# A fp32 decoder trunk: contiguous compression operand, all weight pieces split by engines, eight pair tiles and four raw tiles

## The chip, the core and the metric

One core of a Trainium2 chip runs the whole kernel in one launch. The metric is the device time in microseconds (us) of one execution. The engines are named as in the profile: PE (TensorE, the matmuls), PEld (its weight loads), DVE (VectorE), ACT (ScalarE), POOL (GpSimd) and SP (SyncE, which here only issues transfers). Each engine works through its own queue of instructions in the order in which they were written; one that waits holds up all behind it on that engine.

## The reference, cut to what matters

The input is one sequence of 256 tokens with 1024 features, all in fp32. Two layers follow one another, each a token mixer and an MLP.

```python
for i in range(DEPTH):                       # DEPTH = 2
    h = _rmsnorm(x, norm_mix[i])
    x = x + (_rglru_mixer(h, ...) if i % 2 == 0 else _nsa_mixer(h, ...))
    h = _rmsnorm(x, norm_ffn[i])
    x = x + _sq_relu_mlp(h, mlp_w_up[i], mlp_w_down[i])
return _rmsnorm(x, norm_final)
```

The first mixer is recurrent (projections, a short convolution, gates, a scan). The second is sparse attention with 16 heads in 4 groups. It has three branches: a compressed one, a selected one and a sliding window. The compressed keys and values come from blocks of 32 tokens, taken every 16 tokens, which gives 15 blocks:

```python
def _compress(z, pe, w1, w2):
    blocks = blocks + pe[None, None, :, None, :]          # a learned offset per position in the block
    flat = ...reshape(B, nc, G, CMP_LEN * DH)             # 32 x 64 numbers per block and group
    return jax.nn.gelu(flat @ w1, approximate=True) @ w2
```

## The kernel before, in words

Activations lie with features on the 128 partitions and the 256 tokens along the free axis. Every large product is made of three matmuls (`mm3`, L327 to L330): weight and activation are each split into a high part in fp32r and a low part, the rounding rest, and high by high, high by low and low by high are summed in a PSUM bank. So every weight must be split before use.

**Pieces.** The weights come as pieces of 128 x 1024 numbers (512 KB), in the order of `weight_pieces`. A piece is loaded from HBM into one of NRAW = 5 raw tiles (`load`, L274, on SP's queue), copied into the high half of one of NSPL = 7 pair tiles (`whl`) by ACT or DVE, and then the low half is written by DVE as raw minus high, a "diff" here (L297 in the MLPs, L333 elsewhere). PE consumes a piece with 24 matmuls. A raw tile is free after the diff, a pair after PE's last matmul of that piece. Eight pieces (`BY_DMA`: q3, kw1, q5, q7, o01, o03, o11, o13) go another way (`split_dma`): POOL's queue loads the piece into the high half (L388), ACT or DVE writes its negative into the low half (L390), and a second load on POOL's queue adds the raw weight to that (L392). They are read from HBM twice and need no raw tile.

**Order.** The two mixers, with the norms around them, are written as tasks (`Plan.add`): engine or engines that may do it, a duration, what it reads and writes. `Plan.plan` makes a list schedule from priorities, improves it with passes forwards and backwards, and `emit` writes the instructions in the order of the planned starts. `SEEDS` holds, for each mixer, the seeds that disturb the priorities. So the order on every engine follows from a table of numbers and the durations in the code. The MLPs are written by hand: at each of their 64 pieces a `tick` makes the diff of one piece and the high copy of the next, up to 6 pieces ahead of PE.

**The attention section** runs from the statistics of the norm (L434 to L445) to those of the next norm. Its pieces are, in order, ks0 kw0 q0 q1 (keys and queries), ck0 ck1 cv0 cv1 (inputs of the compression), q2, five pieces of values, q3 ks1 kw1 q4 q5 q6 q7, and o00 to o13 (output). A projection (`proj`, 24 matmuls) is multiplied by the norm's factor into a scratch tile `tt`. Keys and queries of ks0, kw0, q0, q1 and q2 are split straight into their places by ACT and DVE; those of the others are split into `th`/`tl` and carried to other partitions by transfers of 64 KB on SP's queue (`move`, L364). Then come, head by head, `scores` (L1149, L1150), the exponentials on ACT (L1159), `rescale` (L1178), `transposes` (L1189) with their split into `pth` (ACT, L1192) and `ptl` (DVE, L1193), and for every two heads `pv` (L1214, L1216, L1221), whose result goes through `osum` (ACT L1225, DVE L1228) to the output projection. There are eight of these pv steps. Every stage has work on PE, ACT and DVE.

**The compression.** `cproj` (L943) copies the scaled projection into a tile `zf`: for each of 15 blocks and 4 groups, 16 positions, with the two halves of the block on the two halves of the partitions. This is done by 16 transfers on SP's queue (tile `zwoh` in the profile). Two more transfers fetch the learned offset as column 60 of each half (L931). `hidden` then multiplies with `w1` (tile `zwol`): 16 matmuls over 122 columns (L957), one per position `l`. `zf` is stored with the position innermost, so that the 122 columns of `zf[:, :, l]` lie 16 numbers (64 bytes) apart. `hidden` goes on with a short chain on ACT and DVE (L963 to L971), whose result `hid` the matmuls L978 and L997 need. `zf` and `w1` lie in the space that the attention's outputs `oh` and `ol` take later.

## Time and profile before

Three runs took 584.11, 585.10 and 585.17 us. One execution was profiled.

| what | us |
|---|---|
| median of the three runs | 585.1 |
| profiled execution | 583.35 |
| its span, first to last instruction | 581.6 |
| recurrent mixer, to the second statistics | about 95 |
| first MLP | about 173 |
| attention section, from 267.6 to 404.8 | 137.2 |
| second MLP and the final norm | about 177 |

The profile lists, for each engine, when it was busy, by line and tile, and what ended its idle time. Times in views are us from the start of the span. In the views by stretch of time, each engine's busy time is followed by its number of instructions. A DVE or ACT instruction is shown from its start to its end, and the next may start some 0.1 us before that end, so the step from start to start in a full queue is a little shorter than the duration shown.

### The profile page before, as it was taken

Reading aid. Unit: us, or ns where it says so; the run is one execution under the profiler, and the core shown is the slowest. Engines: PE = TensorE matmul, PEld = TensorE weight load, DVE = VectorE, ACT = ScalarE, POOL = GpSimd, SP = SyncE. Lnnn points to the kernel's source line nnn. Section 1 sums busy time; section 2 is a strip of 40 time slices with the busy share of each in tenths; the row PEclk is TensorE's granted clock in tenths of the full one; section 3 lists DMA queues with packets and bytes.
Section 4 is the critical chain, followed back from the end, with each engine's and each line's share of the span. In section 5 each row is a group of like instructions: output and inputs, shape, how many; then the busy total and the mean of one; then the engine's idle time right before and its main releaser. Section 6 shows DMA issues by size and latency. Waiting matters only on the chain.

```text
span 581.6 us, 12202 instructions
## 1 busy us (share of the span) xinstructions
PE 568.7 (98%) x4766; PEld 559.3 (96%) x4766; DVE 416.3 (72%) x859; ACT 356.9 (61%) x715; POOL 54.4 (9%) x69
## 2 busy tenths in 40 slices
PE   9999999999999999999999999999999999999994
PEld 9999999999999999999999988989999999999994
DVE  6999998776775646648749989999867766464522
ACT  7699776666564434437528999987866654443410
POOL 1110000000001113111011100000000000232320
PEclk9999999999999999999999999999999999999998
DMA  8936466565665664665597776333766667466302
GB/s 295 382 126 206 142 224 223 185 206 186 191 207 186 204 220 158 205 219 202 130 308 176 162 187 173 133 74 98 254 193 190 199 193 240 160 194 229 122 1 72
DMA packets 34761, 108.39 MB, mean 186 GB/s; under 512 B 4592, under 2 KB 8576, under 8 KB 34704
## 3 DMA queue, kind: packets, MB, share of 16 engines
q1 hardware_dynamic: 31776, 98.61, 52.1%
q0 software_dynamic: 2352, 8.49, 6.8%
q8 instruction: 37, 0.61, 0.4%
q10 hardware_dynamic: 576, 0.53, 0.3%
q14 instruction: 20, 0.16, 0.1%
HBM read 103.48 MB, written 1.05 MB: 180 GB/s over the span
## 4 chain that ended last, share of the span: by engine, by line
PE 88%; ACT 5%; DVE 4%; DMA 2%; issue 1%; POOL 0%; DVEq 0%; ACTq 0%; POOLq 0%
PE bank L329 27%; PE bank L328 27%; PE bank L330 27%; PE bank L689 2%; ACT pt L1159 2%; DMA whl<-in_dram 2%; ACT pt L1178 1%; PE bank L574 1%; PE bank L1189 1%; ACT pth L1192 1%; DVE whl L333 1%; DVE ptl L1193 1%; DVE pt L1156 1%; PE bank L1149 0%; PE bank L1150 0%
## 5 line engine op out<-in xcount | busy, mean ns | idle before, releaser
L328 PE MATMUL bank<-hhl,whl 128*128 128x256 f32 x768 | 215.0, 280 | 0.2 <-DVE tt L893 0.2
L329 PE MATMUL bank<-hhl,whl 128*128 128x256 f32 x768 | 212.6, 277 | 0.0
L330 PE MATMUL bank<-hhl,whl 128*128 128x256 f32 x768 | 212.4, 277 | 0.0
L297 DVE TENSOR_TENSOR whl<-raw,whl 128x1024 fp32r<-128x1024 f32 x118 | 147.5, 1271 | 2.8 <-ACT whl L288 2.8
L328 PEld LDWEIGHTS bank<-hhl,whl 128*128 128x128 f32 x768 | 144.2, 188 | 0.7 <-DVE tt L893 0.4
L329 PEld LDWEIGHTS bank<-hhl,whl 128*128 128x128 f32 x768 | 144.3, 188 | 0.5 <-DVE hhl L582 0.2
L330 PEld LDWEIGHTS bank<-hhl,whl 128*128 128x128 f32 x768 | 144.2, 188 | 0.0
L328 PE MATMUL bank<-uhl,whl 128*128 128x256 f32 x512 | 141.4, 276 | 0.0
L330 PE MATMUL bank<-uhl,whl 128*128 128x256 f32 x512 | 141.3, 276 | 0.0
L329 PE MATMUL bank<-uhl,whl 128*128 128x256 f32 x512 | 141.3, 276 | 0.0
L288 ACT CAST whl<-raw 128x1024 fp32r<-128x1024 f32 x119 | 121.2, 1041 | 23.4 <-issue 18.8
L329 PEld LDWEIGHTS bank<-uhl,whl 128*128 128x128 f32 x512 | 96.1, 188 | 0.0
L330 PEld LDWEIGHTS bank<-uhl,whl 128*128 128x128 f32 x512 | 96.1, 188 | 0.0
L328 PEld LDWEIGHTS bank<-uhl,whl 128*128 128x128 f32 x512 | 96.1, 188 | 0.0
L532 DVE TENSOR_TENSOR xt<-xt,bank 128x256 f32<-128x256 f32 x40 | 16.1, 416 | 84.5 <-PE bank L330 84.4
L333 DVE TENSOR_TENSOR whl<-raw,whl 128x1024 fp32r<-128x1024 f32 (+3 forms) x64 | 66.3, 1058 | 3.9 <-ACT whl L336 3.9
L784 ACT ACTIVATE u<-t 128x256 f32<-128x256 f32 x64 | 26.7, 418 | 57.3 <-DVE t L779 54.1
L336 ACT CAST whl<-raw 128x1024 fp32r<-128x1024 f32 (+3 forms) x57 | 52.6, 947 | 11.1 <-DMA raw<-in_dram 6.7
L779 DVE SCALAR_TENSOR_TENSOR t<-bank,rstd 128x256 f32<-128x256 f32 x64 | 26.9, 423 | 45.3 <-PE bank L330 44.8
L1317 ACT ACTIVATE xg<-xt,vec 128x256 f32<-128x256 f32 x8 | 4.1, 509 | 47.9 <-DVE xt L532 47.9
L1159 ACT ACTIVATE pt<-pt,mx 128x256 f32<-128x256 f32 (+1 forms) x64 | 28.6, 450 | 3.4 <-DVE mx L1156 3.3
L508 ACT ACTIVATE hhl<-xt,vec 128x256 fp32r<-128x256 f32 x8 | 4.1, 510 | 39.3 <-DVE xt L532 39.3
(207 smaller groups left out, 821.0 us busy)
## 6 DMA issues: line engine op xcount, KB each, us to landing
raw<-in_dram SPq DMA_DIRECT2D x167, 512.0 KB, 4.3
whl<-in_dram POOLq DMA_DIRECT2D x16, 512.0 KB, 5.7
gw<-in_dram SPq DMA_DIRECT2D x4, 512.0 KB, 9.0
raw<-in_dram SPq DMA_DIRECT2D x5, 256.0 KB, 4.7
xt<-in_dram SPq DMA_DIRECT2D x4, 256.0 KB, 4.5
zwol<-in_dram SPq DMA_DIRECT2D x2, 512.0 KB, 6.3
zwoh<-tt SPq DMA_DIRECT2D x16, 60.0 KB, 2.3
raw<-in_dram SPq DMA_DIRECT2D x2, 456.0 KB, 4.9
```

Of the source, the lines that this page charges most:

```text
L288: (act.copy if eng is None else eng.tensor_copy)(hi_t[i % NSPL][:, :n], raw_t[i % NRAW][:, :n])
L297: (eng or dve).tensor_tensor(lo[:, :n], raw_t[i % NRAW][:, :n], hi[:, :n].bitcast(F32), op=OP.subtract)
L328: pe.matmul(ps, wh, xh, start=start, stop=False)
L329: pe.matmul(ps, wh, xl, start=False, stop=False)
L330: pe.matmul(ps, wl, xh, start=False, stop=stop)
L333: return lambda e: e.tensor_tensor(o, a, h.bitcast(F32), op=OP.subtract)
L336: return lambda e: (e.copy if e is act else e.tensor_copy)(o, a)
L532: dve.tensor_tensor(xt[:, m], xt[:, m], z, op=OP.add)
L689: e.matmul(z(), gw[b][:, o:o + P], xb[2 * b + k], start=k == 0, stop=k == 1)
L779: dve.scalar_tensor_tensor(t, z, 0.0, rs, op0=OP.max, op1=OP.mult)
L784: act.activation(u, t, AF.Square)
L1159: add("act", (0.39, 0.49)[qc], lambda e, row=row, j=j: e.activation(row, row, AF.Exp, bias=mx[:, j:j + 1], scale=-1.0, accum_out=sm[:, j:j ...
```

## The change

- `zf` is stored with the block innermost: the 122 columns that a matmul of `hidden` reads lie side by side. The 16 transfers of `cproj` become copies on ACT or DVE, whose writes are now 122 numbers apart, and the two transfers of the learned offset become copies on POOL.
- `BY_DMA` and `split_dma` are gone: all pieces are loaded on SP's queue and split by ACT and DVE.
- Four raw tiles instead of five, eight pair tiles instead of seven. Two pieces, q3 and ks1 (`LENT`), get no pair: their halves lie in the `oh` and `ol` tiles, which the compression has left by then and pv needs later. The scratch tiles `tt`, `gx` and `gy` are replaced by tiles that exist already.
- The planner knows transfers as a task on SP that issues (0.6 us) and a task on one "dma" resource that carries them in the order of issue; of its three best plans it takes the one whose replay, with queues in fixed order, ends PE first. Two costs in `stats` are raised, and both tables of seeds are new.

```diff
-NRAW, NSPL = 5, 7
+NRAW, NSPL = 4, 8
...
-BY_DMA, DLEAD, NPEN = "q3 kw1 q5 q7 o01 o03 o11 o13", 8.0, 0.3
-MLAG = (3.4, 4.0)
+LENT = "q3 ks1".split()
+TRANSFER = {"raw": (2.0, 1.4, 0.6), "move": (1.4, 0.21, 0.3)}
...
-FIRST = "x0+ 00 01 x2+ 10+ 20+ x4+ 02+ x6+ 12+ 22+ piece vec cst piece"
+FIRST = "x0+ 00 01 x2+ 10+ 20+ x4+ 02+ x6+ 12+ 22+ piece vec cst"
...
     def plan(self, prio):
         plans = [self.list_schedule(prio, 0.1)]
         for _ in range(ROUNDS):
             plans.append(self.forwards(self.backwards(*plans[-1])))
-        return min(plans, key=lambda p: max(p[0].values()))
+        plans.sort(key=lambda p: max(p[0].values()))
+        return min(plans[:3], key=lambda p: self.replay(*p))
...
-        while state["dma"] <= min(i + 4, len(order) - 1):
+        while state["dma"] <= min(i + NRAW - 1, len(order) - 1):
...
+        def transfer(self, kind, q, d, fn, t, r=(), w=()):
+
+            pre, took, post = TRANSFER[kind]
+            self.add(q, d, fn, r=r, w=list(w) + ["loads"] * (kind == "raw"), t=t, lag=pre)
+            self.plan.carried[len(self.plan.tasks)] = len(self.plan.tasks) - 1
+            self.add("dma", took, lambda e: None, r=r, w=w, t=t, lag=post)
...
-                if j in by_dma:
-                    continue
-                self.add("sp", 1.5, lambda e, j=j: load(j), w=[("raw", j % NRAW), "loads"], t=t - 20 + j * 1e-3, lag=2.0)
+                self.transfer("raw", "sp", 0.6, lambda e, j=j: load(j), t - 20 + j * 1e-3, w=[("raw", j % NRAW)])
...
-        def split_dma(self, i, n, hi, lo, t):
-
-            src = wts[offs[i]:offs[i + 1]].rearrange("(p n) -> p n", p=P)
-            hk, lk = [("hi", i % NSPL)], [("lo", i % NSPL)]
-            self.add("pool", 0.6, lambda e: e.dma_start(hi, src), w=hk, t=t - DLEAD, lag=4.8)
...
+        def slot(self, i):
+
+            if home[i] >= 0:
+                return hi_t[home[i]], lo_t[home[i]], [("hi", home[i])], [("lo", home[i])]
+            b = home[i] + 2
+            return Lent("oh", b), Lent("ol", b), [("oh", 4 * b + j) for j in range(4)], [("ol", 4 * b + j) for j in range(4)]
...
-        tt = many([P, S], F32, "tt", 3)
+        tt, ttk = [acc, *sqs], ["acc", ("sq", 0), ("sq", 1)]
...
-        zf = zw[0][:, :2 * ZW * 16].rearrange("p (z l) -> p z l", l=16)
+        zf = zw[0][:, :2 * ZW * 16].rearrange("p (l z) -> p z l", l=16)
...
-            add("sp", 0.5, lambda e, i=i, c=pecol: e.dma_start(zf[:, ZW * i + 60], vec_in[:, c:c + 16]), r=zok,
-                w=[("z", i, "p")], t=W1T, lag=2.0)
+            add("pool", 0.15, lambda e, i=i, c=pecol: e.tensor_copy(zf[:, ZW * i + 60], vec[:, c:c + 16]), r=zok + ["vec"],
+                w=[("z", i, "p")], t=-5)
...
-                    dst = zf[own_(j), ZW * i + g * NB:ZW * i + (g + 1) * NB].rearrange("p n l -> p (n l)")
-                    sec.move(dst, x[own_(hf), j * 16:j * 16 + 240], [xk] + zok, [("z", i, g, j)], t + 0.5, "sp")
+                    dst = zf[own_(j), ZW * i + g * NB:ZW * i + (g + 1) * NB]
+                    y = x[own_(hf), j * 16:j * 16 + 240].rearrange("p (n l) -> p n l", l=16)
+                    add(HI, copy(dst, y), r=[xk] + zok, w=[("z", i, g, j)], t=t + 0.5)
```

Three places show how the order moves. The first is SP's queue in the first third of the attention section. `raw` tiles receive weights, `zwoh` is the tile of `zf`, `sa`, `sb`, `kh` and `kl` are queries and keys that are carried from `th` and `tl`. Before:

```order
L274 DMA raw_79<-in_dram 128x1024
L364 DMA zwoh<-tt_3227 64x240 x4
L364 DMA zwoh<-tt_3225 64x240 x4
L364 DMA zwoh<-tt_3226 64x240 x4
L364 DMA zwoh<-tt_3227 64x240 x4
L274 DMA raw_81<-in_dram 128x1024
L274 DMA raw_78<-in_dram 128x1024
```

After the change, at the same place:

```order
L312 DMA raw_80<-in_dram 128x1024
L312 DMA raw_81<-in_dram 128x1024
L312 DMA raw_78<-in_dram 128x1024
L415 DMA sb_3217<-th_3223 64x256
L415 DMA sa_3213<-th_3223 64x256
L415 DMA sb_3217<-tl_3225 64x256
L415 DMA sa_3213<-tl_3225 64x256
L415 DMA kh<-th_3224 64x256 x4
L312 DMA raw_79<-in_dram 128x1024
```

The 16 transfers into `zwoh` are gone; loads of raw weights follow one another up to the first transfers of queries.

The second place is PE's queue around the 16 matmuls of `hidden` (L957, now L1004). `bank_3608` and `bank_3623` hold values before, `bank_3565` holds the projection q2 after. Before:

```order
L1019 MATMUL bank_3608<-whl,hhl 128x304
L1020 MATMUL bank_3608<-whl,hhl 128x304
L1021 MATMUL bank_3608<-whl,hhl 128x304
L957 MATMUL bank_3652<-zwoh,zwol 128x122 x16
L1019 MATMUL bank_3623<-whl,hhl 128x304
L1020 MATMUL bank_3623<-whl,hhl 128x304
```

After:

```order
L366 MATMUL bank_3565<-hhl,whl 128x256
L367 MATMUL bank_3565<-hhl,whl 128x256
L368 MATMUL bank_3565<-hhl,whl 128x256
L1004 MATMUL bank_3593<-zwoh,zwol 128x122 x16
L366 MATMUL bank_3565<-hhl,whl 128x256
L367 MATMUL bank_3565<-hhl,whl 128x256
```

Ahead of `hidden`, PE had all of q2 (24 matmuls), 30 matmuls of values and five pairs of score matmuls before; now it has 18 matmuls of q2, none of values and four pairs of scores. The seven projections ahead of q2 stand there as before.

The third place is ACT's queue where `hidden` has ended (`cb`, L963, now L1010). Before:

```order
L336 CAST sa_3214<-tt_3225 64x256
L336 CAST whl<-raw_81 128x1024
L963 COPY cb<-bank_3652 64x1 x2
L336 CAST whl<-raw_78 128x1024
L969 ACTIVATE gy<-gy 128x60
```

After:

```order
L374 CAST whl<-raw_79 128x1024
L1206 ACTIVATE pt,sm_3246<-pt,mx_3242 128x128
L374 CAST oh<-raw_80 128x1024
L1010 COPY cb<-bank_3593 64x1 x2
L374 CAST sb_3216<-acc 64x256
L374 CAST sa_3212<-acc 64x256
L1016 ACTIVATE cs_3250<-cs_3250 128x60
```

The high half of a lent piece is written to `oh`, the tile of `zf`, right ahead of `cb`, and no cast of a piece stands between `cb` and the tanh (L969, now L1016).

More of the change, by code (lines that the diff above doesn't have):

```diff
@@ L118, in lag @@
         lag = self.tasks[i][4]
-        if lag is not None and not by == e == "sp":
+        if lag is not None and by != e:
             return lag
@@ L218, in priorities, with replay @@
         return prio
+    def replay(self, end, by, dur, work=lambda i, e, d: d, wait=lambda i, l: l):
+        queues = {e: [] for e in self.engines}
+        for i in sorted(end, key=lambda i: (round(end[i] - dur[i], 6), i)):
+            queues[by[i]].append(i)
+        carrier = {u: i for i, u in self.carried.items()}
+        free, done, head = dict(self.busy), {}, {e: 0 for e in queues if e != "dma"}
+        ready = dict.fromkeys(head)
+        while True:
+            for e, r in ready.items():
+                if r is None and head[e] < len(queues[e]):
+                    i = queues[e][head[e]]
+                    if all(k in done for k in self.tasks[i][2]):
+                        ready[e] = max([free[e]] + [done[k] + wait(k, self.lag(k, by[k], e)) for k in self.tasks[i][2]]), e, i
+            left = [r for r in ready.values() if r]
+            if not left:
+                break
+            t, e, i = min(left)
+            ready[e] = None
+            head[e] += 1
+            free[e] = done[i] = t + work(i, e, dur[i])
+            if i in carrier:
+                u = carrier[i]
+                t = max([free["dma"]] + [done[k] + wait(k, self.lag(k, by[k], "dma")) for k in self.tasks[u][2]])
+                free["dma"] = done[u] = t + work(u, "dma", dur[u])
+        assert len(done) == len(end)
+        return max(t for i, t in done.items() if by[i] == "pe")
     def plan(self, prio):
@@ L262, in trunk_kernel @@
     state = {"dma": 0, "split": 0, "lo": 0, "get": 0}
+    home, lent, n = {}, {}, 0
+    for i, x in enumerate(order):
+        if x[0] + str(x[1]) in LENT:
+            home[i] = LENT.index(x[0] + str(x[1])) % 2 - 2
+        else:
+            home[i], n = n % NSPL, n + 1
     WMAX = 1024
@@ L341, in trunk_kernel, with __init__, __getitem__ @@
     piece_no = {n: i for i, n in enumerate(order)}
-    by_dma = {piece_no[x[:-1], int(x[-1])] for x in BY_DMA.split()}
+    class Lent:
+        def __init__(self, name, b):
+            self.name, self.b = name, b
+        def __getitem__(self, at):
+            return lent[self.name](self.b)[at]
     class Section:
@@ L407, in ahead @@
             for i in range(g, min(g + n, len(order))):
-                self.add("pe", 2.58, lambda e: None, r=[("hi", i % NSPL), ("lo", i % NSPL)] + ["rs"] * (i - g >= 2),
+                self.add("pe", 2.58, lambda e: None, r=[("hi", home[i]), ("lo", home[i])] + ["rs"] * (i - g >= 2),
                          w=["next"], t=t + step * (i - g))
-            self.load(g + n + 3, t)
+            self.load(g + n + NRAW - 2, t)
         def bank(self, key, b, view):
@@ L674, in gate_load @@
             o = offs[-1] + b * P * 1024
-            add("sp", 1.5, lambda e: e.dma_start(gw[b], wts[o:o + P * 1024].rearrange("(p n) -> p n", p=P)), w=[("gw", b), "loads"],
-                t=t, lag=2.0)
+            sec.transfer("raw", "sp", 0.6, lambda e: e.dma_start(gw[b], wts[o:o + P * 1024].rearrange("(p n) -> p n", p=P)), t,
+                         w=[("gw", b)])
         def gate(b, t):
@@ L854, in trunk_kernel, with lend @@
         oh, ol = (lambda i, n=n: opart(n, i) for n in ("oh", "ol"))
+        def lend(n):
+            return lambda b: (opart(n, 0), ohl[n][:, b * WMAX:(b + 1) * WMAX])[1]
+        lent.update({n: lend(n) for n in ("oh", "ol")})
         ptht, ptlt = (at.tile([P, NTH * 3 * P], F32R, name=n) for n in ("pth", "ptl"))
@@ L924, in trunk_kernel @@
         hid = pre.tile([P, 4, NCP], F32, name="hid")
-        gx, gy = (pre.tile([P, 60], F32, name=n) for n in ("gx", "gy"))
         GELU1, GELU3 = float(np.sqrt(2.0 / np.pi)), 0.044715
@@ L959, in hidden @@
             t += 3
-            x, y, k2 = gx, gy, ["gx"]
+            (x, y), k2 = (c.rearrange("p j q n -> p (j q n)")[:, :60] for c in css), [("cs", 0), ("cs", 1)]
             for i in range(2):
```

52 lines of the change are left out of this document (23 added, 29 removed).

## The prediction

> **What bounds the kernel now.** I read the page first, then the stretches of the attention section, then what VectorE and SP wait for in it.
>
> ```profile
> span 581.6 us, 12202 instructions
> PE 568.7 (98%) x4766; PEld 559.3 (96%) x4766; DVE 416.3 (72%) x859; ACT 356.9 (61%) x715; POOL 54.4 (9%) x69
> ```
>
> PE is busy in 98% of the span, so only the stages in which it waits, or does slow work, can give anything. Busy time by stretch, PE first, then PEld, DVE, ACT and POOL:
>
> ```profile
> 30.00:60.00 30.00, 30.00 (x216) 28.55 (x215) 29.51 (x49) 29.56 (x54) 2.11 (x5) 1.00 0.52 173
> 105.00:245.00 140.00, 140.00 (x1238) 140.00 (x1237) 89.67 (x120) 72.50 (x112) 13.15 (x11) 1.00 0.60 196
> 267.60:305.00 37.40, 36.94 (x279) 36.30 (x276) 24.82 (x60) 19.83 (x47) 3.46 (x5) 1.00 0.79 240
> 305.00:390.10 85.10, 81.72 (x615) 75.42 (x616) 80.50 (x315) 79.67 (x245) 8.54 (x15) 1.00 0.60 149
> 390.10:404.80 14.70, 14.70 (x131) 14.67 (x131) 14.45 (x33) 9.74 (x21) 0.00 (x0) 1.00 0.33 96
> 410.00:568.00 158.00, 158.00 (x1396) 158.00 (x1396) 92.56 (x122) 77.78 (x121) 18.76 (x13) 1.00 0.57 177
> ```
>
> In the MLPs (second and last row) a matmul takes 140/1238 = 0.113 us, PE never rests, and DVE has a third of its time free. They give nothing. The three rows between them are the attention section: 137.2 us, cut where `hid` is made (305.0) and where the last pv has left `osum` (390.1). From 305 on, DVE rests 85.1 - 80.5 = 4.6 us, ACT 5.4 us and PE 3.4 us: all three are nearly full and wait on each other in turn. Ahead of 305, DVE rests 12.6 us. Where this rest lies, by DVE's own stretches, and what ends it:
>
> ```profile
> 281.00:289.80 8.80, 6.59 (x19) 1.00 0.44 92
> 289.80:305.00 15.20, 6.57 (x14) 1.00 1.02 317
> ```
>
> ```profile
> 276.51 0.33 SPq L274 DMA_DIRECT2D raw<-in_dram  x1
> 278.26 11.44 SPq L364 DMA_DIRECT2D zwoh<-tt  x16
> 289.80 2.67 SPq L274 DMA_DIRECT2D raw<-in_dram  x5
> ```
>
> ```profile
> DVE whl L390 <- DMA whl<-in_dram: 5.8, 2, 5.5
> ```
>
> From 276.5 to 289.8 SP issues only the 16 transfers of the compression; no weight is loaded, and then five loads and those of POOL come at once. In the last 15.2 us DVE works 6.57 us; 5.8 us of its rest are one wait for a piece that POOL's queue loads.
>
> **The change, part by part.** All terms are taken against the profiled execution, 583.35 us with a span of 581.6; it lies 1.75 us under the median of 585.1, and I add the same difference to the median.
>
> *The operand of `hidden`.*
>
> ```profile
> L957 PEld LDWEIGHTS bank<-zwoh,zwol x32: 192/206/207, 293.8 to 300.1; 128*128 128x128 f32 x32
> L957 PE MATMUL bank<-zwoh,zwol x32: 372/384/386, 293.9 to 300.3; 128*128 128x122 f32 x32
> L689 PE MATMUL bank<-xb,gw x64: 378/379/379, 27.2 to 47.0; 128*128 128x256 f32 x64
> L997 PE MATMUL bank<-w2raw,pt x8: 218/275/275, 306.9 to 307.6; 128*128 128x64 f32 x8
> ```
>
> The 16 matmuls are 32 records, (300.3 - 293.9)/31 = 0.206 us each. For a contiguous fp32 operand there are two rows: 256 columns end 0.379 us after their start, as late as these 122; and 64 columns follow one another in 0.7/7 = 0.10 us. So 122 contiguous columns should take between 0.10 and some 0.12 us; I take 0.11, and 32 x (0.206 - 0.11) = 3.1 us leave PE. The bounds are 2.7 and 3.4.
>
> [...]
>
> *The copies into `zf`.* There are 16, ten on ACT and six on DVE by the order.
>
> ```profile
> L336 ACT COPY pt<-hid 128x128 f32<-128x128 f32 x2 | 0.6, 293 | 0.0
> L336 DVE COPY pt<-hid 128x128 f32<-128x128 f32 x2 | 0.4, 220 | 0.0
> ```
>
> The nearest copies have 128 numbers per partition, these 240. I take 0.32 us on ACT and 0.27 on DVE: 3.2 and 1.6 us. They can't cost less than the quoted rows, and with writes at twice the price they cost 6.4 and 3.2. The last of them stand between cv1's projection and `hidden`: one on ACT, three on DVE. Meanwhile PE has a pair of scores and 18 matmuls of q2, 2.2 us. At my price DVE needs 0.4 + 3 x 0.27 = 1.2 us, and PE doesn't wait; at twice the price it takes 2.0 and is just in time.
>
> *Eight pieces by engines.* Eight more diffs on DVE. The eight negations (L390, five on ACT, three on DVE) become eight high copies of about the same length.
>
> ```profile
> 363.30 1.14 DVE whl L333
> ...
> 368.87 1.14 DVE whl L333
> ```
>
> ```profile
> L390 ACT ACTIVATE whl<-whl x5: 1047/1052/1064, 310.9 to 353.8; 128x1024 fp32r<-128x1024 f32 x5
> L390 DVE TENSOR_SCALAR whl<-whl x3: 679/695/699, 291.8 to 382.5; 128x1024 fp32r<-128x1024 f32 x3
> ```
>
> DVE: 8 x 1.14 = 9.1 more, 1.6 of copies, 3 negations of 0.6 less, and 1.2 less since the order gives small copies to ACT: +7.7 us. By the order there are 10 diffs before `hid` in both kernels, then 7 before and 15 now up to the last pv, then 4 in both. So about 0.2 of this falls ahead of `hid` and 7.5 between `hid` and the last pv. ACT gets about +6.8, of which 4 after `hid`: 79.7 + 4 = 83.7, less than DVE's 88.0. DVE is the one to watch.
>
> *How early `hid` is made.* PE's order puts L957 ahead of 30 matmuls of values (0.14 us each, 4.2), 6 of q2 (0.7) and a pair of scores (0.2). It starts at 293.9 - 5.1 = 288.8 and ends 16 x 2 x 0.11 = 3.5 later, at 292.3. What follows `hidden` before:
>
> ```profile
> 301.68 1.05 ACT L336 CAST whl<-raw 128x1024 fp32r<-128x1024 f32 x1 [0.59 <-ACT cb L963]
> ```
>
> ```profile
> 301.86 0.70 DVE L390 TENSOR_SCALAR whl<-whl 128x1024 fp32r<-128x1024 f32 x1 [5.51 <-DMA whl<-in_dram]
> 302.47 0.57 DVE L965 TENSOR_SCALAR gx<-bank,cb 64x60 f32<-64x60 f32 x2
> ...
> 303.47 1.22 DVE L333 TENSOR_TENSOR whl<-raw,whl 128x1024 fp32r<-128x1024 f32 x1
> ...
> 305.00 0.21 DVE L971 SCALAR_TENSOR_TENSOR hid<-gy,gx 128x60 f32<-128x60 f32 x1
> ```
>
> From L965 to the end of L971 it was 2.7 us with a diff of 1.2 in between; now two diffs of 0.34 stand there, so 2.2. Ahead of it ACT now writes the lent piece into `oh`, which must wait for `hidden` to leave that space: 1.0 us, and 0.3 for `cb`. So `hid` comes at 292.3 + 0.1 + 1.0 + 0.3 + 2.2 = 295.9. Counted from 267.6 that is 28.3; I take 28.5 instead of 37.4. DVE has 24.8 + 0.2 = 25.0 us of work there, so it fits, with 3.5 us of rest instead of 12.6.
>
> *Transfers.* The wait for L390 goes, 4 MB are read less, and the 16 transfers no longer stand ahead of loads on SP. In the middle, one stall is a queue of transfers:
>
> ```profile
> 339.00:348.00 9.00, 7.73 (x61) 7.23 (x60) 7.34 (x24) 8.03 (x23) 1.42 (x2) 1.00 0.59 133
> ```
>
> ```profile
> 338.85 0.24 PE bank L1189 x3
> 339.08 1.79 DMA sb<-th
> 340.87 0.28 DVE th L336
> ...
> 341.83 0.53 PE bank L1189 x3
> ```
>
> Here DVE rests 9.0 - 7.34 = 1.7 us of its 4.6. With POOL's loads gone and transfers planned in the order of issue I let this one go: 2.9 us of rest remain.
>
> *Four raw tiles, eight pairs, borrowed tiles.* At nothing, since loads stay far ahead:
>
> ```profile
> L297 DVE TENSOR_TENSOR whl<-raw,whl 128x1024 fp32r<-128x1024 f32 x118 | 147.5, 1271 | 2.8 <-ACT whl L288 2.8
> ...
> raw<-in_dram SPq DMA_DIRECT2D x167, 512.0 KB, 4.3
> ```
>
> ```profile
> DMA to landing us min/median/max: 3.1/4.3/11.0
> ```
>
> In an MLP load i+3 starts when diff i-1 is done (1.27 after tick i) and must land by tick i+3, 3 x 24 x 0.113 = 8.1 us after tick i. That leaves 6.9 us for a landing of 4.3, and PE is up to six pieces behind the splits. If the cover went, each piece would cost the excess. The recurrent mixer is planned anew on engines that are 98% busy (first row of stretches); PE never waits there before, so it can only lose: 0 to 1 us, I take 0.
>
> **The sum.** DVE's work and rest fill the section: 28.5 to `hid`, then 80.5 + 7.5 + 2.9 = 90.9, then 14.5 as before: 133.9 instead of 137.2, 3.3 us less. PE alone would allow 133.4 - 3.1 = 130.3. Profiled 580.05, median **581.8 us**. One measurement of this kernel can tell about 0.2%, 1.2 us, from no change.
>
> **The rivals.** *PE stays the bound.* The new order packs DVE without rest and `hid` comes in time: only PE's 130.3 counts, 6.9 us less, 578.2. For it: all the diffs that were added have pieces loaded early. Against it: PE, ACT and DVE then need 95% and more of the same time.
>
> *A wait takes the place of the old ones.* The stall of 339 is replaced by another, since eight more loads share SP's queue with the 64 KB transfers (rest 4.6), and the copies into `zf` at twice the price bring `hid` to 30: 30 + 88.0 + 4.6 + 14.5 = 137.1, no change, 585.0. [...]
>
> *Four raw tiles are too few* (slower). A tile's round is landing, high copy (1.05), diff (1.2). With four tiles it must stay under 4 x 2.71 = 10.8, so it decides at a landing of 8.5 us. The longest landing is 11.0; at 9.6 each piece costs 0.25 us, and 25 diffs up to the last pv cost 6.3: 3 us slower than before with the gain of 3.3 taken off, 588.1. For it: DMA share 1.02 in 289.8 to 305. Against it: this crowd came from loads held back by the 16 transfers, and the median is 4.3.
>
> **How the numbers follow.** Forecast 0.45; PE the bound 0.23; another wait 0.17; four tiles 0.15. The forecast's own range is 580.4 to 583.5 (a rest of 1.5 to 4.6 us behind the same `hid`), all of it faster by over 0.2%. So faster 0.68, same 0.17, slower 0.15. The range of 577.5 to 586.3 leaves out most of the slower case and the best end of PE's.
>
> **What would show it.** L1004's records at about 0.11 us; `hid` at about 296; no load held back between 276 and 290; DVE resting 2 to 4 us from `hid` to the last pv, the section 134 long, the MLPs unchanged. I am wrong if PE's rate in the MLPs changes, if `hid` comes after 300, or if DVE rests more than 6 us behind it.

## The result, and the profile after

The changed kernel takes 592.84 us (median, 592.52 to 594.71), the kernel before 584.61 (583.60 to 585.17) on the same chip: a ratio of 1.0149, with a 95% interval of 1.0137 to 1.0161. It is 8.2 us slower, where 2.8 to 3.3 us faster was forecast. The profiled execution after took 593.09 us, with a span of 591.3; the one before has 581.6. So 9.7 us are to be found between the two traces, 1.5 us more than between the medians, since the profiled execution before (583.35 us) is a short one.

The page of the changed kernel, its first lines:

```profile
span 591.3 us, 12174 instructions
PE 569.8 (96%) x4766; PEld 559.6 (95%) x4766; DVE 428.3 (72%) x869; ACT 366.8 (62%) x729; POOL 43.2 (7%) x55
```

PE was busy in 98% of the span before, now in 96%: it waits for 21.5 us instead of 12.9. Where the time went can be cut at ACT's copy of rstd, which opens each section (start of the last three of its four copies, us from the span's start):

| | 2nd (MLP 0) | 3rd (attention) | 4th (MLP 1) | span |
|---|---|---|---|---|
| before | 95.1 | 267.9 | 404.9 | 581.6 |
| after | 99.8 | 274.1 | 414.5 | 591.3 |
| lost up to here | 4.7 | 6.3 | 9.6 | 9.7 |

The recurrent mixer lost 4.7 us, the step from there into the attention 1.6, the attention 3.3 and the rest nothing. The same stretches of the changed kernel that the prediction quoted of the kernel before, and two more at the starts of sections (busy time of PE, PEld, DVE, ACT and POOL, then granted clock, DMA share and GB/s):

```profile
24.40:30.00 5.60, 4.54 (x36) 4.24 (x36) 5.54 (x19) 3.75 (x8) 0.98 (x3) 1.00 1.02 415
105.00:245.00 140.00, 140.00 (x1238) 140.00 (x1237) 90.70 (x127) 75.79 (x123) 11.30 (x10) 1.00 0.61 199
268.00:274.50 6.50, 4.18 (x35) 3.80 (x33) 2.31 (x4) 3.17 (x5) 0.79 (x3) 1.00 0.66 213
274.50:305.00 30.50, 29.33 (x231) 28.83 (x231) 26.83 (x60) 23.90 (x52) 0.00 (x0) 0.94 0.49 152
305.00:397.00 92.00, 88.26 (x665) 82.25 (x664) 88.08 (x322) 86.41 (x257) 1.63 (x4) 1.00 0.38 110
397.00:414.50 17.50, 16.02 (x120) 15.47 (x121) 14.40 (x32) 9.81 (x22) 0.00 (x0) 0.90 0.45 154
```

The MLP's rate is unchanged (1238 matmuls in 140 us). `hid` is made 30.5 us behind rstd instead of 37, as hoped, but the stretch behind it grew from 85.1 to 92.0 and the tail from 14.7 to 17.5. PE is the engine to follow: in the attention it was busy for 36.94 + 81.72 + 14.70 = 133.4 us before, and for 29.33 + 88.26 + 16.02 = 133.6 now, although the operand of `hidden` saves it 3 us. The granted clock, third from the right in a row, tells why: 0.94 over 30.5 us and 0.90 over 17.5 us leave 1.8 + 1.8 = 3.6 us of full clock missing, an estimate from these rows. Without that PE's work would be 130.0 us, close to the 130.3 that the prediction has for PE alone. The rest of the loss is waits: PE rests for 140.0 - 133.6 = 6.4 us of the section, 3.8 before. The operand does what it should:

```profile
L1004 PE MATMUL bank<-zwoh,zwol x32: 275/275/343, 297.4 to 300.9; 128*128 128x122 f32 x32
```

(300.9 - 297.4)/31 = 0.113 us for one record instead of 0.206. The largest new wait is at the attention's start. ACT's instructions there, first before, then after:

```profile
267.86 0.37 ACT L445 COPY rstd<-bank 128x256 f32<-128x256 f32 x1 [0.76 <-PE bank L529]
268.72 2.33 ACT L336 CAST kh<-tt 64x256 fp32r<-64x256 f32 x6 [0.49 <-DVE tt L893]
271.08 1.05 ACT L336 CAST whl<-raw 128x1024 fp32r<-128x1024 f32 x1
```

```profile
269.85 0.26 ACT L484 ACTIVATE rcol<-bank,epst 128x2 f32<-128x2 f32 x1 [0.25 <-PE bank L567]
273.19 1.05 ACT L374 CAST whl<-raw 128x1024 fp32r<-128x1024 f32 x1 [3.08 <-DMA raw<-in_dram]
274.14 0.36 ACT L488 COPY rstd<-bank 128x256 f32<-128x256 f32 x1
```

Now a high copy of a weight piece stands between the root and the copy of rstd. It is q2's piece, which is multiplied only behind the eight projections of the compression, but ACT works its queue in order: it waits 3.08 us for that piece, and rstd waits with it. Why the piece is late stands in the waits of SP's queue between 262 and 275 (total, times, longest), and in the landing times of line 312 between 264 and 276:

```profile
SPq L312 <- DVE whl L335: 7.2, 1, 7.2
...
DMA to landing us min/median/max: 4.0/5.4/6.9
```

The transfer itself took 4.0 us. It was issued only at 269.1, since SP waited 7.2 us for a diff to free the tile. Before, a load waited as long between 255 and 275, but no high copy that needs it stood ahead of rstd:

```profile
SPq L274 <- DVE whl L297: 10.7, 4, 7.2
```

Behind rstd hang VectorE (its timeline, first fence) and then PE, which gets a lower clock when it comes back (stretches, second fence):

```profile
274.54 0.42 DVE L940 TENSOR_TENSOR sq<-bank,rstd 128x256 f32<-128x256 f32 x1 [4.23 <-ACT rstd L488]
```

```profile
275.00:277.00 2.00, 1.99 (x9) 1.99 (x10) 2.00 (x2) 1.61 (x4) 0.00 (x0) 0.50 0.59 227
397.40:400.00 2.60, 2.52 (x11) 2.33 (x12) 2.21 (x4) 1.40 (x3) 0.00 (x0) 0.58 0.45 178
```

Nine matmuls in 2.0 us, 0.22 us each, at a granted clock of 0.50. The second row lies behind the other large wait, the one behind the last pv. PE's timeline there, first before, where nothing waits, then after:

```profile
388.49 0.40 PE L1221 MATMUL bank<-pc,bhl 128*128 128x256 f32 x2
388.72 0.28 PE L328 MATMUL bank<-oh,whl 128*128 128x256 f32 x1
```

```profile
394.95 0.40 PE L1268 MATMUL bank<-pc,bhl 128*128 128x256 f32 x2
397.40 0.38 PE L366 MATMUL bank<-oh,whl 128*128 128x256 f32 x1 [2.04 <-DVE oh L374]
```

### The profile page after: what moved, and what is told of

Same layout as the page of the kernel before. It is cut to its first block, busy times and chain, and to the rows that moved or that the text cites. A ratio compares the mean times of both kernels' runs of the same rounds, so it can differ in the third digit from the quotient of the medians.

```text
span 591.3 us, 12174 instructions
## 1 busy us (share of the span) xinstructions
PE 569.8 (96%) x4766; PEld 559.6 (95%) x4766; DVE 428.3 (72%) x869; ACT 366.8 (62%) x729; POOL 43.2 (7%) x55
## 4 chain that ended last, share of the span: by engine, by line
PE 81%; ACT 7%; DVE 6%; DMA 4%; issue 1%; SPq 0%; DVEq 0%; ACTq 0%
PE bank L366 24%; PE bank L367 24%; PE bank L368 24%; DMA raw<-in_dram 3%; PE bank L732 2%; ACT pt L1206 2%; ACT whl L374 1%; ACT zwoh L374 1%; ACT pt L1225 1%; PE bank L1236 1%; PE bank L1263 1%; DVE whl L371 1%; PE bank L1004 1%; ACT pth L1239 1%; DMA vec<-in_dram 1%
## 5 line engine op out<-in xcount | busy, mean ns | idle before, releaser
L366 PE MATMUL bank<-hhl,whl 128*128 128x256 f32 x752 | 211.3, 281 | 2.8 <-DVE sq L940 2.8
L367 PE MATMUL bank<-hhl,whl 128*128 128x256 f32 x752 | 209.0, 278 | 3.2 <-DVE hhl L625 2.6
L368 PE MATMUL bank<-hhl,whl 128*128 128x256 f32 x752 | 208.7, 278 | 0.0
L367 PEld LDWEIGHTS bank<-hhl,whl 128*128 128x128 f32 x752 | 142.0, 189 | 4.0 <-DVE hhl L625 2.8
L366 PEld LDWEIGHTS bank<-hhl,whl 128*128 128x128 f32 x752 | 142.0, 189 | 3.3 <-DVE sq L940 3.0
L368 PEld LDWEIGHTS bank<-hhl,whl 128*128 128x128 f32 x752 | 141.9, 189 | 0.0
L371 DVE TENSOR_TENSOR whl<-raw,whl 128x1024 fp32r<-128x1024 f32 (+3 forms) x70 | 74.1, 1074 | 4.1 <-ACT whl L374 3.8
L374 ACT CAST whl<-raw 128x1024 fp32r<-128x1024 f32 (+3 forms) x60 | 57.8, 971 | 14.9 <-DMA raw<-in_dram 12.2
L1206 ACT ACTIVATE pt<-pt,mx 128x128 f32<-128x128 f32 (+1 forms) x64 | 28.7, 451 | 2.8 <-DVE mx L1203 2.5
```

What stands on the lines that cost most here:

```text
L366: pe.matmul(ps, wh, xh, start=start, stop=False)
L367: pe.matmul(ps, wh, xl, start=False, stop=False)
L368: pe.matmul(ps, wl, xh, start=False, stop=stop)
L371: return lambda e: e.tensor_tensor(o, a, h.bitcast(F32), op=OP.subtract)
L374: return lambda e: (e.copy if e is act else e.tensor_copy)(o, a)
L1206: add("act", (0.39, 0.49)[qc], lambda e, row=row, j=j: e.activation(row, row, AF.Exp, bias=mx[:, j:j + 1], scale=-1.0, accum_out=sm[:, j:j ...
```

## The experiments

Three theories stood against each other. *Theory 1*: the four raw tiles make loads late, and casts wait in front of what others need. *Theory 2*: the new order of instructions gives the time away, whatever the loads do. *Theory 3*, the prediction's own: VectorE sets the pace of the attention. "With five tiles" below means a_raw5, on which later runs are built.

| run | median us | against before, 95% interval |
|---|---|---|
| after | 592.84 | 1.0149 (1.0137 to 1.0161) |
| a_raw5 | 587.29 | 1.0038 (1.0020 to 1.0057) |
| a_rsfirst | 588.67 | 1.0067 (1.0046 to 1.0087) |
| a_nolo | 594.37 | 1.0165 (1.0137 to 1.0192) |
| b_contig | 585.50 | 1.0010 (0.9989 to 1.0030) |
| r5_next | 586.07 | 1.0025 (1.0012 to 1.0037) |
| r5_cover | 586.49 | 1.0035 (1.0008 to 1.0062) |
| r5_loops | 587.30 | 1.0035 (1.0023 to 1.0048) |
| r5_start | 586.95 | 1.0025 (1.0013 to 1.0037) |
| b_pool | 582.25 | 0.9954 (0.9938 to 0.9971) |
| b_poolmix | 582.15 | 0.9958 (0.9944 to 0.9973) |
| r5_pool | 593.09 | 1.0147 (1.0130 to 1.0164) |
| s_best | 591.19 | 1.0109 (1.0094 to 1.0124) |
| s_order | 583.79 | 1.0007 (0.9979 to 1.0035) |

The runs were taken in groups, each with its own runs of the kernel before, whose medians lie between 584.2 and 585.0 us. The ratio is taken against these, so medians of two groups can differ by some tenths of a us by that alone.

### A fifth raw tile, nothing else moved (a_raw5)

```diff
-    raw_t = [rpool.tile([P, WMAX], F32, name="raw%d" % i) for i in range(NRAW)]
+    raws = [rpool.tile([P, WMAX], F32, name="raw%d" % i) for i in range(5)]
+    raw_t = [raws[i % 5 if i < 100 else (i - 100) % NRAW] for i in range(len(order))]
-        th, tl = many([P, S], F32R, "th", 2), many([P, S], F32R, "tl", 2)
+        th, tl = ([raws[4][:, o:o + S].bitcast(F32R) for o in (a, a + S)] for a in (0, 2 * S))
```

> The changed kernel with every instruction in its place, but a fifth raw tile under the loads up to the hundredth piece (the tiles th and tl of the attention, used later, lie in it), so that a load waits for the difference of the piece five before it and not four. Late loads (theory 1: the four raw tiles make loads land late and casts that stand first in ACT's and DVE's queues wait for them): the stall of 2.9 us at 272 goes, with the slow matmuls behind it (about 1.3), and the 1.2 us wait for the gates at 27 and some 0.8 us more in the recurrent mixer: 586.5 to 588.5 us. The order (theory 2: the time was lost where the new order of instructions puts work in front of other work, whatever the loads do): 592 to 593, no change. If the stall of 2.7 us at 6.9 comes from the load rotation too, 584 to 586.

Measured: 587.29 us, 5.6 less by the medians and 1.1% by the ratios, as the first case had it. ACT's timeline at the attention's start, and the stretch with the gates' first products:

```profile
268.19 1.04 ACT L375 CAST whl<-raw 128x1024 fp32r<-128x1024 f32 x1
269.75 0.37 ACT L489 COPY rstd<-bank 128x256 f32<-128x256 f32 x1 [0.52 <-PE bank L573]
```

```profile
24.40:30.00 5.60, 5.60 (x41) 5.29 (x40) 5.37 (x18) 3.93 (x7) 0.57 (x2) 1.00 0.84 327
```

The same cast in the same place no longer waits, rstd comes at 269.75 instead of 274.14, and PE's rest between 24.4 and 30 (5.60 - 4.54 = 1.06 us after) is gone. Theory 1 holds for the larger part of the loss. What it does not explain: 0.38% is left against before. The executions of a_raw5 fall in two groups by their mean granted clock: two at 0.995 took 585.7 us, five at 0.990 to 0.993 took 587.2 to 589.0. The median lies in the second group, the profiled execution (585.67 us) in the first. Where the clock fell stands in the last section.

### The late cast behind rstd (a_rsfirst)

```diff
+        for a, b in self.behind:              # (cast of q2's piece, copy of rstd)
+            line.remove(a)
+            line.insert(line.index(b) + 1, a)
```

> The changed kernel with one instruction moved: ACT's cast of the piece for q2, which stood ahead of the copy of rstd at the start of the attention, stands behind it. If this one place is what the attention lost at its start: the 2.9 us stall of TensorE at 272 and the slow matmuls behind it go, 588.5 to 590 us. If DVE has too much work behind the compression to let anything that is won at the start through (theory 3: DVE sets the pace of the attention): 592 to 593.

Measured: 588.67 us, at the low end of the first case. ACT's timeline at the same place:

```profile
271.85 0.37 ACT L494 COPY rstd<-bank 128x256 f32<-128x256 f32 x1 [1.46 <-PE bank L578]
273.31 1.05 ACT L379 CAST whl<-raw 128x1024 fp32r<-128x1024 f32 x1 [1.10 <-DMA raw<-in_dram]
```

The load is as late as ever; only nobody waits for it. So one instruction's place is worth about 4 us, the wait and the low clock behind it, and the two causes need each other: the fourth tile made the load late, the order put its cast in front of rstd. Either repair alone removes this wait.

### Eight us less work on VectorE (a_nolo)

```diff
-    self.add("dve", 1.14, lambda e: diff(lo[:, :n], rw[:, :n], hi[:, :n])(e), ...)
+    skip = order[i][0] + str(order[i][1]) in "kw1 q5 q7 o01 o03 o11 o13".split()
+    self.add("dve", 1.14, lambda e: skip or diff(lo[:, :n], rw[:, :n], hi[:, :n])(e), ...)
```

> The changed kernel without the DVE differences (the low parts) of the seven pieces kw1, q5, q7, o01, o03, o11 and o13, so that low parts left in their tiles are multiplied; everything else in its place. DVE loses 7 x 1.14 = 8 us of work, all behind the compression. DVE sets the pace there (theory 3): 5 to 8 us less, 585 to 588 us. The order and its chains of single waits decide (theory 2): 0 to 2 us less, 591 to 593.

Measured: 594.37 us, no less than after. The stretch from `hid` to the last pv, first after, then without those diffs:

```profile
305.00:396.90 91.90, 88.26 (x665) 82.25 (x664) 87.98 (x322) 86.31 (x257) 1.63 (x4) 1.00 0.38 110
```

```profile
304.70:396.40 91.70, 87.95 (x665) 82.00 (x664) 82.01 (x316) 85.87 (x257) 1.64 (x4) 1.00 0.38 111
```

VectorE has 6 us less to do in it, rests 9.7 us instead of 3.9, and the stretch is 0.2 us shorter. Theory 3 falls: in this order VectorE does not set the pace. PE does, with 88 us of work, and what it waits for is single results.

### The contiguous operand alone (b_contig, b_pool, b_poolmix)

These are the kernel before, in its own order. Where the planner put a transfer into `zf`, a copy is issued.

```diff
-        zf = zw[0][:, :2 * ZW * 16].rearrange("p (z l) -> p z l", l=16)
+        zf = zw[0][:, :2 * ZW * 16].rearrange("p (l z) -> p z l", l=16)
...
-                    sec.move(dst, x[own_(hf), j * 16:j * 16 + 240], [xk] + zok, [("z", i, g, j)], t + 0.5, "sp")
+                    add("sp", 0.6, lambda e, d=dst, y=y, q=(act, dve)[j]: copy(d, y)(q), ...)   # b_pool: q=pool
```

> The kernel before with its order kept, and the contiguous operand alone: the 16 transfers into the operand are 16 copies at the same places of the order, 8 on ACT and 8 on DVE, and the position column is copied by GpSimd. As the prediction has it for this part: 32 matmuls (16 pairs of passes) at 0.11 instead of 0.206 us, some 3 us of TensorE, and the copies beside other work: 581 to 583 us. The copies cost as much as they bring (16 x 0.3 us on the two engines that everything waits for): 584 to 587. DVE sets the pace behind the compression, so that a hidden product that ends 3 us earlier still brings its 3 us: 581.5.

Measured: 585.50 us, not told apart from before, as the second case had it. `hidden` has 0.113 us a record, as after, but a new wait of PE stands ahead of it. VectorE in the middle of the projections of the compression, and 8 us of all engines there, first before, then here (PE 8.00 us busy, then 5.83):

```profile
287.48 0.59 DVE L336 COPY zwoh<-tt 64x240 f32<-64x240 f32 x1
288.10 1.23 DVE L333 TENSOR_TENSOR whl<-raw,whl 128x1024 fp32r<-128x1024 f32 x1
289.36 0.56 DVE L336 COPY zwoh<-tt 64x240 f32<-64x240 f32 x1
289.95 0.42 DVE L1158 CUSTOM_DVE_ANT_0 pt<-bank,cst 128x256 f32<-128x256 f32 x1
```

```profile
284.00:292.00 8.00, 8.00 (x66) 7.91 (x65) 5.99 (x20) 3.55 (x14) 0.57 (x1) 1.00 0.66 162
284.00:292.00 8.00, 5.83 (x49) 5.58 (x48) 7.77 (x17) 3.98 (x8) 0.57 (x1) 1.00 0.63 209
```

A copy takes 0.6 us, not 0.27, and PE waits 2.2 us for a bank that L1158 behind the copies must empty. Behind this wait the clock is at half for 3.3 us, which takes another 1.6 us, an estimate:

```profile
292.00:295.30 3.30, 3.30 (x17) 3.30 (x16) 1.84 (x9) 3.02 (x11) 0.00 (x0) 0.50 1.07 413
```

So the wait and the clock together take back what the operand gives. If that is the price of the operand, an engine with nothing else to do should give the gain back:

> The kernel before with its order, the contiguous operand, and the 16 copies into it on GpSimd, which has little else to do there (with these copies on ACT and DVE it took 585.5 us, with a new stall of 2.3 us of TensorE at 288 behind copies and differences on DVE). If the operand's 3 us were lost to copies that stand in ACT's and DVE's queues: the stall is gone, and 581.5 to 582.5 us. If GpSimd needs over 1 us for a copy, the last four land 4 us late and the hidden product waits for them: 584.5 to 586. If the chain behind the compression sets the end whatever the hidden product does: 584.5.

> As the run beside it, but the last four copies are on ACT and DVE (two each, written in runs of 15 side by side, 0.62 and 0.37 us), so that nothing waits for GpSimd at the end. If GpSimd is too slow for the last copies: 1 to 3 us less than the run beside it; if it isn't: the same within 0.5 us. Against before: 581.5 to 582.5 us if the queues of ACT and DVE were the cost of the copies, 584.5 if the chain behind sets the end.

Measured: 582.25 and 582.15 us. The same 8 us, and the sections of b_pool up to `hid`, to the last pv and to rstd:

```profile
284.00:292.00 8.00, 8.00 (x66) 7.86 (x66) 6.01 (x19) 4.36 (x15) 7.60 (x11) 1.00 0.80 274
...
268.90:302.40 33.50, 33.29 (x274) 32.86 (x273) 25.91 (x61) 19.49 (x47) 16.57 (x21) 1.00 0.70 222
302.40:389.30 86.90, 82.85 (x622) 75.98 (x621) 80.92 (x316) 80.09 (x245) 8.90 (x16) 1.00 0.62 150
389.30:404.00 14.70, 14.70 (x131) 14.65 (x130) 14.08 (x32) 9.78 (x22) 0.00 (x0) 1.00 0.31 97
```

PE rests for only 0.2 us ahead of `hid`, and the attention is 2 us shorter than before. So the operand is worth its 2.5 us where its copies stand in nobody's way; moving the last four copies off GpSimd changes nothing. This is the fastest version of the study, 0.46% (0.29 to 0.62) faster than before.

### The wait behind the last pv (r5_next, r5_cover)

A section's plan ends with placeholders (the method `ahead`): tasks of 2.58 us on PE for pieces of the next section, with no instruction behind them. In the plan of before, the three of the attention start behind the fourth rstd; in that of the change, two start ahead of it (planned us):

```
before: placeholders at 135.92, 139.18, 141.76; rstd done at 135.70
change: placeholders at 121.58, 131.16, 141.24; rstd done at 140.34; last pv on PE until 121.58
```

So the plan has PE at work behind the last pv where the chip shows it waiting 2.0 us. r5_next makes the placeholders read the banks of the section's last matmuls, which puts them behind; r5_cover moves real matmuls into the gap.

```diff
# r5_next
-    r=[("hi", home[i]), ("lo", home[i])] + ["rs"] * (i - g >= 2),
+    r=[("hi", home[i]), ("lo", home[i])] + ["rs"] * (i - g >= 2) + [("ps", b) for b in (0, 1, 2, 6)],
# r5_cover
-    z = zview(("out", half, m), b, zcols)
+    z = zview(("out", half, m), 5 if (half, m) == (1, 5) else b, zcols)
+    # two of its three groups are issued straight behind the last pv
```

> With five raw tiles (as in the run before), and one rule of the planner mended: the placeholders by which a section's plan holds TensorE for the next section's first pieces, 2.58 us each, with no instruction behind them, may stand only behind the section's own matmuls. In the changed kernel's plan one stands behind the last weighted-values product and one among the last output projections, both ahead of the fourth rstd; in the plan of before all three stand behind it. Same numbers of the search; the planner moves other work where the placeholders were. Theory 2 (the order gives away time where the plan has a placeholder and the chip has nothing): the 2.2 us stall of TensorE behind the last product goes, and the plan's rstd comes 1.7 us sooner: 585 to 585.8 us against 587.3. Rival: the chain of scores, exponentials and transposes sets that stall, and it stays or moves ahead of the product: 587 to 588.

> With five raw tiles, and two matmul groups moved by hand (9 matmuls, 1.0 us: the first three quarters of the sixth output projection of the second half, into a bank of its own): from behind the other five to straight behind the last weighted-values product, where TensorE waits 2.2 us. If that stall only lacks work to stand in it (theory 2): 1.0 us less and a little for the clock, 585.8 to 586.3. If what follows waits for the same chain and not for TensorE: 587 to 587.5.

Measured: 586.07 and 586.49 us against 587.29; neither is told apart from a_raw5, whose interval overlaps theirs. Their traces show what happened. In r5_cover, by PE's timeline, the wait behind the last pv shrinks to 0.98, and the next one, for a chunk of the norm, grows to 1.68 from 0.69 in a_raw5:

```profile
391.47 0.39 PE L372 MATMUL bank<-oh,whl 128*128 128x256 f32 x1 [0.98 <-DVE oh L380]
...
401.03 0.39 PE L373 MATMUL bank<-hhl,whl 128*128 128x256 f32 x1 [1.68 <-DVE hhl L501]
```

In r5_next the wait is gone, but PE waits ahead of the last pv for probabilities that ACT scales (0.5 and 0.3 us), and osum's last two additions come 2.4 us later than in a_raw5 (392.8 instead of 390.4). Some 1.7 of these 2.4 us, an estimate, are the clock: r5_next's profile has it at 0.50 from 302.7 to 306.1, a_raw5's does not. Taken at like clock, 0.994 and more, r5_next took 585.1 to 586.4 us and r5_cover 585.4 to 586.0, a_raw5 585.7. Neither brings the 1 to 1.7 us that theory 2 forecast for it, so the rival fits better: the end of the attention is one chain (exponentials, scaling, transposes, pv, `oh`, projection, norm). In these two runs, work put into its gaps moved them and did not close them. The placeholders hid this from the plan; that they cost time by themselves is not shown.

### Two smaller suspects (r5_loops, r5_start)

```diff
# r5_loops: both views of a copy into the operand in the other order
-    dst = zf[...]                      ; y = x[...].rearrange("p (n l) -> p n l", l=16)
+    dst = zf[...].rearrange("p n l -> p l n") ; y = x[...].rearrange("p (n l) -> p l n", l=16)
# r5_start: two casts on DVE behind hl of x's third chunk, one matmul group on PE forward
```

> With five raw tiles, and the 16 copies into the contiguous operand written with their two free dimensions in the other order, so that each run of 15 elements is written side by side and read 64 bytes apart; before, it was read side by side and written 244 bytes apart. The profile has 0.64 us on ACT and 0.59 on DVE for one of them, twice the 0.32 and 0.27 of the prediction. If the far writes double it: 0.32 and 0.27 now, and the hidden product, which waits 1.0 us for the last copies, starts 0.6 to 1 us sooner: 586.3 to 586.8 us against 587.3. If strided reading costs as much: 0.6 again and 587.3.

> With five raw tiles, and three instructions at the kernel's start moved: on DVE two casts that wait for a weight load stand behind the low part of the third chunk of x, not ahead of it, and on TensorE the fourth chunk's products of the first piece follow the third's. If order alone makes the startup's stalls of 2.4 us: 0.6 to 1 us less, 586.3 to 586.7. If the late landing of the loads does: 587.3.

Measured: 587.30 and 586.95 us, both inside a_raw5's interval. (In the first expectation the distance of the writes is a slip: it is 122 numbers, 488 bytes.) The copies with runs of 15 numbers side by side, in the groups of r5_loops:

```profile
L375 ACT COPY zwoh<-sq 64x240 f32<-64x240 f32 x6 | 3.7, 618 | 0.1
...
L375 DVE COPY zwoh<-sq 64x240 f32<-64x240 f32 x6 | 2.2, 370 | 0.1
```

VectorE gains (0.59 to 0.37 us), ACT doesn't (0.64 to 0.62). The last copy is now one on ACT, from 291.0 on, and `hidden` starts at 291.7, as in a_raw5 (291.6). At the start, between 5 and 12 us, PE's work rises from 4.99 us in a_raw5 to 6.31 (before 7.00), so order does matter there; but one us is less than these runs can tell. The loads of the start also land differently from run to run: the one issued at 2.6 us landed at 7.1 in the profile of before, but at 8.0 in b_contig and 8.2 in b_pool, whose start is the same program, and these two have 6.33 and 6.17 us of PE's work between 5 and 12. So 0.7 to 0.8 of the 2.0 us by which a_raw5 falls short of before there goes with the early landing in that one execution. How much of the rest is order stays open.

### The changed kernel with its copies on GpSimd, and searched anew (r5_pool, s_best, s_order)

r5_pool issues the 16 copies on GpSimd in a_raw5's order. s_best lets the planner know of the fifth tile, mends the placeholders, has the copies on GpSimd at 0.68 us, and both orders come from a new search with the kernel's own planner (seeds only). s_order is the same with the copies at measured prices on whichever engine the planner likes:

```diff
-    add(HI, copy(dst, y), r=[xk] + zok, w=[("z", i, g, j)], t=t + 0.5)
+    add([("act", 0.62, 0.0), ("dve", 0.4, 0.0), ("pool", 0.95, 0.0)], copy(dst, y), r=[xk] + zok, ...)
```

> The changed kernel in its own order with five raw tiles, and the 16 copies into the operand on GpSimd, as in the version of the kernel before that was faster. ACT loses 10 x 0.64 us and DVE 6 x 0.59 us ahead of the hidden product. If these copies in the queues of the two engines are what makes TensorE wait 1.0 us for the product and 0.5 us around it: 585.8 to 586.5 us against 587.3. If the last four copies in one queue, 4 x 0.64 = 2.6 us, come later than now: 587.5 to 588.5.

> The changed kernel with all that was found to cost: five raw tiles that the planner knows of up to the hundredth piece, placeholders only behind a section's own matmuls, copies on GpSimd at 0.68 us, and the order of both planned sections searched anew by the kernel's own planner under these rules (its forecast for the attention is 1.8 us less than with the mended placeholders alone). Lost time lies in these four things: 584 to 584.6 us, no slower than before. The design itself (more differences and casts on DVE and ACT behind the compression) is what can't be packed: 586 to 587.

> The changed kernel with five raw tiles that the planner knows of, placeholders only behind a section's own matmuls, the copies into the operand at the prices that the runs showed (0.62 us on ACT, 0.4 on DVE, 0.95 on GpSimd, each where the planner puts it, in runs of 15 side by side), and both planned sections searched anew by the kernel's own planner. Its forecast for the attention is 1.2 us less than with the mended placeholders alone. What is left of the loss (587.3 with five raw tiles) lies in the order: 584 to 585 us. It lies in the design, more casts and differences on ACT and DVE between the compression and the last product, whatever the order: 586 to 587.

Measured: 593.09, 591.19 and 583.79 us. The first two were worse than either case that I had written. The tile of the operand in r5_pool:

```profile
L1005 PE MATMUL bank<-zwoh,zwol x32: 275/378/426, 295.7 to 300.9; 128*128 128x122 f32 x32
L375 POOL COPY zwoh<-sq x12: 591/642/1494, 281.5 to 295.1; 64x240 f32<-64x240 f32 x12
L375 POOL COPY zwoh<-acc x4: 624/993/1565, 284.5 to 288.2; 64x240 f32<-64x240 f32 x4
```

A copy takes about 0.64 us by itself and up to 1.57 beside a weight's diff on VectorE (see the last section). All 16 last from 281.5 to 295.7, and `hidden`, which the change put straight behind the projections, waits for them from 291 on. In the kernel before, `hidden` stood behind 38 other matmuls (30 of values, 6 of q2 and two of scores), so that there the same copies were hidden. GpSimd is no remedy for the changed order, and s_best, whose plan has them at 0.68 us, has the same wait of PE, 4.1 us.

s_order is free of that. Its attention, up to `hid`, to the last pv and to rstd:

```profile
269.30:300.60 31.30, 31.09 (x255) 30.46 (x253) 28.68 (x62) 22.10 (x49) 5.45 (x7) 1.00 0.53 176
300.60:390.00 89.40, 86.04 (x647) 79.81 (x647) 85.25 (x315) 86.02 (x258) 0.58 (x4) 1.00 0.39 112
390.00:405.00 15.00, 14.92 (x132) 14.73 (x131) 13.64 (x31) 9.62 (x21) 0.00 (x0) 1.00 0.30 93
```

It is not told apart from before (1.0007, 0.9979 to 1.0035). So nearly all that the change lost can be had back by a fifth raw tile, true prices and a new order, with the splits by engines kept: PE's rests in the attention are 135.7 - 132.05 = 3.7 us, against 137.2 - 133.4 = 3.8 before. What s_order does not show is a gain. b_pool, which has the operand but not the splits by engines, is 2.5 us faster than before. Whether the splits cost s_order that gain stays open, and which of its mendings did most was not taken apart.

## Why the prediction was wrong, point by point

The profiled span was forecast 3.3 us shorter than before and came 9.7 longer, so 13.0 us are missing: 4.7 in the recurrent mixer and 1.6 at the step into the attention, both put at nothing, and 6.6 in the attention, half of them a gain that did not come (0.1 lies behind). Two steps failed, the load term of the four raw tiles and the sum that goes by VectorE.

- **The operand of `hidden`**: right. 0.11 us a record was forecast, 0.113 measured.
- **The copies into `zf`**: mis-sized. The term was 0.32 us on ACT and 0.27 on VectorE, from contiguous copies; they took 0.64 and 0.59. The plan behind the changed order had them at 0.31 and 0.21 (`HI` in the kernel), and the order was packed by that. The text had "twice the price" as a bound, where it still calls PE just in time; PE waited 0.7 us, for ACT's last copy, where the text had counted VectorE's. The factor of two was an estimate, which no quoted row of the kernel before shows. In r5_loops, with 15 numbers written side by side and read 64 bytes apart, a copy took 0.37 us on VectorE instead of 0.59, and 0.62 on ACT instead of 0.64. So on VectorE the order of writes and reads makes 0.22 us of the 0.59; what makes ACT's 0.64 is not shown.
- **`hid` at about 296**: mis-sized. Counted from the start of rstd's copy, 28.2 us were forecast and 30.8 came. PE's wait for the copies is 0.7 of the difference, the half clock behind rstd some 1.7, an estimate; in a_raw5, with full clock there, it is 29.5. And rstd itself came 6.3 us later than before, so that `hid` came at 305.0 as before.
- **"DVE's work and rest fill the section"**: this step failed. The sum had the right length for the stretch behind `hid` (90.9 forecast, 92.0 measured), and its terms came true as well (88.0 of work forecast and 88.1 measured, 2.9 and 3.9 of rest), but that is luck, since VectorE does not hold the stretch: six us less on it changed its length by 0.2 (a_nolo). The stretch is long because PE's work that no longer stands ahead of `hid` stands behind it: 665 matmuls instead of 615, 88.26 us instead of 82. For PE nothing is gained by an early `hid`; its section is its work plus its waits.
- **"Four raw tiles ... At nothing, since loads stay far ahead"**: this step failed with the largest price, 5.6 us. The argument held for the MLP's steady run, where loads do stay ahead (140 us unchanged). It did not look at the seams between sections, where a tile came free only when VectorE got to the last diffs (SP waited 7.2 us for one), nor at what stands behind a late cast in ACT's queue.
- **Recurrent mixer "0 to 1 us, I take 0"**: mis-sized; 4.7 us were lost, of which a_raw5 takes 1.8 back. 2.0 of the rest are PE's rest between 5 and 12 us, where the profile of before has none and that of b_pool, the same program there, has 0.8.
- **"then 14.5 as before"**: mis-sized; 17.5, with the wait of 2.0 us behind the last pv and the half clock behind that.
- **The rivals**: "four raw tiles are too few" had the right sign and cause and the wrong place: it priced a landing over 8.5 us in the steady run, and the load that hurt landed in 4.0 us, issued late. "PE stays the bound" was right about the engine, but its 130.3 us are work alone, and PE's waits grew from 3.8 to 6.4. "A wait takes the place of the old ones" had the price of the copies and `hid` (30, measured 30.8), but its wait in a transfer; the waits that cost were for rstd and for the last `oh`. The condition named for being wrong, `hid` after 300, came true.

## What to carry to other kernels

Price the seams: at the end of a section look in each in-order queue for an instruction that waits for a transfer, and ask who stands behind it (here rstd, behind a cast that waited 3.08 us); in the steady run the same buffers may look plentiful (here the MLP's 140 us were unchanged). When one engine is busy for 98% of the span, count its work and its waits, one by one, and take no other engine's load for the pace until leaving work out there has changed the time (here 6 us less on VectorE changed the stretch by 0.2). Here the gain on the busy engine was kept where the copies that pay for it stood in a queue that nothing waited for (b_pool, 582.25 us), and not where something did (b_contig 585.50, r5_pool 593.09). And before two versions within half a per cent are compared, look at the granted clock of each execution (a_raw5: 585.7 us at 0.995, 587.2 to 589.0 at 0.990 to 0.993).

## What the runs showed of the hardware that I had not expected

- A wait of PE cost more than its length, but not every time. Behind the wait of 2.8 us at 272 the granted clock was 0.50 (nine matmuls in 2.0 us), behind that of 2.0 us at 395 it was 0.58 over 2.6 us. Cut finer, the trace has the clock at 0.50 from 274.9 to 278.3 and from 397.8 to 401.2, 3.4 us each, so each costs some 1.7 us on top of the wait, an estimate. But in a_raw5 an equal wait of 2.0 us at 389 was followed by a clock of 1.00, and in r5_start, whose order is the same there, by 0.51 (first a_raw5, then r5_start):

```profile
391.20:407.40 16.20, 14.73 (x122) 14.17 (x123) 14.25 (x32) 10.10 (x22) 0.00 (x0) 1.00 0.48 168
393.30:396.80 3.50, 3.50 (x19) 3.50 (x18) 2.71 (x6) 3.21 (x7) 0.00 (x0) 0.51 0.24 44
```

  The execution of r5_start took 587.26 us, that of a_raw5 585.67. All executions of a_raw5 and the four runs r5_next, r5_cover, r5_loops and r5_start divide like this: those at a mean granted clock of 0.994 or more took 585.1 to 586.4 us, those at 0.993 or less 586.5 to 589.0, and one 593.3. So some 1.6 of the 2.3 us that a_raw5's median still loses against before go with this clock, an estimate from these times. What decides whether a wait is followed by half the clock is not shown. The length of the wait is not all: in r5_next the half clock came at 302.7 with no wait of PE over 0.3 us in the 3.4 us ahead of it.
- GpSimd and VectorE were slower beside each other. In b_pool two diffs on VectorE took 2.80 us beside GpSimd's copies, where the same two took 2.35 before (first before, then b_pool). And all five of the 16 copies that took over 1 us, up to 1.5 instead of 0.64, run beside such a diff:

```profile
283.76 2.35 DVE L333 TENSOR_TENSOR whl<-raw,whl 128x1024 fp32r<-128x1024 f32 x2
284.60 2.80 DVE L333 TENSOR_TENSOR whl<-raw,whl 128x1024 fp32r<-128x1024 f32 x2
```

  What makes them slower is not shown.
